# A residual accumulator loaded in four quarters, each at its own step, in the down projection of a transformer-like layer

## The chip, the cores and the metric

The kernel runs on one core of a Trainium2 chip. The core has a matrix engine (TensorE, PE in the profile), a vector engine (VectorE, DVE), a scalar engine (ScalarE, ACT), a general engine (GpSimd, POOL) and a queue engine (SyncE, SP) that issues transfers to sixteen DMA engines. Each engine runs its own list of instructions in order and waits on semaphores for the others. The metric is the device time of one execution in microseconds (us); lower is better.

## The reference, cut to what matters

One layer on 1024 tokens of 1024 channels. The mixing half (attention, a short convolution, a gated block) gives `h`; the change lies in the last lines, the second matrix product of the MLP and the final norm.

```python
x = x + jnp.einsum('bse,ed->bsd', mixed, w_out[l])          # h, 1024 x 1024
hdn = jnp.einsum('bsd,df->bsf', rms_norm(x, mlp_norm_g[l]), w_up[l])
hdn = jnp.square(jax.nn.relu(hdn))                           # 1024 x 4096
x = x + jnp.einsum('bsf,fd->bsd', hdn, w_down[l])            # the down stage
return rms_norm(x, final_norm_g)
```

## The kernel before

**Arithmetic.** Every fp32 product is made of three matmuls of split operands: each operand is written as a high and a low part (`split`, lines 51 to 53: ACT copies the high part, DVE subtracts to get the low part), and `mm3` (lines 63 to 66) adds high by high (L64), high by low of the moving operand (L65) and low of the stationary operand by high (L66).

**The down stage.** The up and down stages use a seven-product scheme (Winograd's form of Strassen) on two by two blocks. In the down stage the hidden layer's 4096 channels are cut into sixteen pairs of 128, and four blocks of four pairs; each block makes seven products in the order of `PLAN` (lines 1185 and 1186), so there are 28 steps. A step's product `m` takes 48 matmuls (4 groups of 128 tokens, 4 pairs, 3 matmuls each) in a PSUM bank of family A or B (`dA`, `dB` in the profile). After each group of tokens `u`, DVE adds the bank into a quarter of the accumulator (line 1220): `(i, k)` names the token half `i` (tiles 4i to 4i+3) and the column half `k` (512 columns). The first seven steps: steps 0 and 1 on quarter (0,0), step 2 (m=6) on (0,1), step 3 (m=5) on (1,1), step 4 (m=7) again on (1,1), step 5 (m=3) again on (0,1), step 6 (m=4) on (1,0).

**Accumulators.** `acc[t]`, eight tiles of 128 x 1024, start as `h`, which an earlier stage wrote to DRAM (`kept[t]`, named `hs` in the profile). `open_acc(t)` (lines 1125 to 1127) loads one tile whole, 512 KB.

**Operands of a step.** `down_ops(m, p)` (lines 1136 to 1154) loads one hidden operand `hr` (256 KB, from `hidden`, `hd..` in the profile), does the block's subtractions on the `w_down` rows `wd` where the product needs them (step 2, m=6: two per pair, `wd<-wd` and `t<-wd,wd`; m=7 and m=4: one), and splits both into `ho` and `wo`. Step 0's operands are made in the stage before. Step 1 needs only the odd rows of `w_down` (`load_down(BLOCKS[0], (1,))`, line 1196); step 2 is the first that needs the even ones. `hr` has 8 buffers, `wd` 10, `ho` and `wo` 10 each, so a new operand waits for the release of an older one.

**The order.** `prep(n + 1)`, the operands of the next step, stands ahead of step n's product in the program. A planner in the language then orders each engine's list ahead of the run by program order and by when it thinks an instruction could start; the SP queue gets its transfers in such an order too. In step 0's turn of the loop come, after `prep(1)`: four accumulator tiles, the even rows of `w_down` of block 0 (four transfers of 512 KB), the other four accumulator tiles, and the gain of the final norm, `gfin`, spread to all partitions (lines 1201 to 1207). `gfin` is first read in the last block (step 25, L1224). In step 4's turn `prep(5)` loads the rows of the second block.

Of the kernel before, what the change touches and what calls it, by code (L numbers as in the profile page):

```python
# [8 lines left out]
F32 = mybir.dt.float32  # L9
# [6 lines left out]
P = 128  # L16
T = 1024
D = 1024
# [12 lines left out]
def trunk(ctx, tc, x, mix_g, w_in, rb_rev, conv_w, sg_ln_g, sg_ln_b, sg_w, sg_b,  # L31
# [3 lines left out]
    load = nc.sync.dma_start  # L35
# [12 lines left out]
    def raw_tile(shape, name):  # L48
        return W.tile(shape, F32, tag="wr", bufs=3, name=name)
# [13 lines left out]
    def mm3(ps, sh, sl, mh, ml, start, stop, **kw):  # L63
        PE.matmul(ps, lhsT=sh, rhs=mh, start=start, stop=False, **kw)  # L64
        PE.matmul(ps, lhsT=sh, rhs=ml, start=False, stop=False, **kw)  # L65
        PE.matmul(ps, lhsT=sl, rhs=mh, start=False, stop=stop, **kw)  # L66
# [32 lines left out]
    def half(hf):  # L99
        return slice(hf * HALF, (hf + 1) * HALF)  # L100
# [49 lines left out]
    n = Rows("n", lambda hf, kp: "N")  # L150
# [3 lines left out]
    class Moving:  # L154
# [7 lines left out]
        def load(self, j):  # L162
            raw = self.raw[j] = raw_tile([P, self.kk, self.m], f"wr_{self.name}{j}")
            rows_ = slice(j * self.kk * P, (j + 1) * self.kk * P)
            load(raw, w_in[rows_, self.c0:self.c0 + self.m].rearrange("(k p) m -> p k m", p=P))
# [557 lines left out]
    for i in range(64):  # L723
        p, k = i // 16, i % 16
# [43 lines left out]
    def bank(name):  # L768
        return psB.tile([P, HALF], F32, tag="b", name=name)
# [49 lines left out]
    xn2, raws, spilled, kept = {}, {}, {}, {}  # L819
# [55 lines left out]
    def add(out, a, b):  # L875
        V.tensor_tensor(out, a, b, op=ALU.add)  # L876
# [127 lines left out]
    class Up:  # L1004
# [5 lines left out]
        def prep(self):  # L1010
            self.ops.raw()
            self.ops.sums()
            return self
# [105 lines left out]
    E_ = ctx.enter_context(tc.tile_pool(name="down", bufs=2, reuse_waits="tile"))  # L1119
    gfin = E_.tile([P, D], F32, tag="gfin", bufs=1, name="gfin")  # L1120
    BLOCKS = [tuple(range(i, i + 4)) for i in range(0, NP, 4)]
    acc = {}
    wd, t2 = {}, {}

    def open_acc(t):
        acc[t] = E_.tile([P, D], F32, tag="acc", bufs=8, name=f"acc{t}")
        load(acc[t], kept[t])

    def load_down(ps, rows=(0, 1)):
        for p in ps:  # L1130
            for i in rows:
                w = E_.tile([P, 2, HALF], F32, tag="wd", bufs=10, name=f"wd{p}{i}")
                load(w, w_down[(2 * p + i) * P:(2 * p + i + 1) * P, :].rearrange("p (k m) -> p k m", k=2))
                wd.setdefault(p, {})[i] = w
# [30 lines left out]
    def early_half(t, k):  # L1165
        square(t, k)
        V.tensor_scalar(sums[t][:, 2:3], sums[t][:, k:k + 1], 1.0 / D, EPS, op0=ALU.mult, op1=ALU.add)

    def finish(t, k):

        ss = sums.get(t)
        square(t, k)
        V.scalar_tensor_tensor(ss[:, 3:4], ss[:, k:k + 1], 1.0 / D, ss[:, 2:3], op0=ALU.mult, op1=ALU.add)  # L1173
        r = sm.tile([P, 1], F32, tag="rf", name="rf")
        G.tensor_tensor(r, ss[:, 3:4], mhalf[:, 0:1], op=ALU.pow)  # L1175
        o = E_.tile([P, D], F32, tag="o", bufs=2, name=f"o{t}")
        for i in (k, 1 - k):
            if t + 1 == NT and i != k:
                A.activation(o[:, half(i)], acc[t][:, half(i)], AF.Copy, scale=r)
            else:  # L1180
                V.scalar_tensor_tensor(o[:, half(i)], acc[t][:, half(i)], r, gfin[:, half(i)], op0=ALU.mult, op1=ALU.mult)
            load(out[t * P:(t + 1) * P, half(i)], o[:, half(i)])
# [15 lines left out]
    for n, (b, s) in enumerate(steps):  # L1198
        if n + 1 < len(steps):
            prep(n + 1)  # L1200
        if n == 0:
            for t in range(4):
                open_acc(t)
            load_down(BLOCKS[0], (0,))
            for t in range(4, 8):
                open_acc(t)
            load(gfin, fin_g.partition_broadcast(P))
        m, which, start, (i, k) = PLAN[s]
        ops = ready.pop(n)
        last = b == len(BLOCKS) - 1  # L1210
        for u in range(4):
            sl = slice(u * P, (u + 1) * P)
            if start:
                banks[which, u] = bank(f"d{which}{u}")
            ps = banks[which, u]
            for j, (ho, wo_) in enumerate(ops):
                mm3(ps, ho[:, 0, sl], ho[:, 1, sl], wo_[:, 0], wo_[:, 1], start and j == 0, j == len(ops) - 1,
                    skip_group_check=True)
            t = 4 * i + u
            add(acc[t][:, half(k)], ps, acc[t][:, half(k)])  # L1220
            if last and m in (2, 7):
                early_half(t, k)
            if last and m == 7 and t + 1 == NT:
                V.tensor_tensor(acc[t][:, half(k)], acc[t][:, half(k)], gfin[:, half(k)], op=ALU.mult)  # L1224
            if last and m in (3, 4):
                finish(t, k)
# [27 lines left out]
```

## Time and profile before

| what | value |
|---|---|
| median of 3 runs | 1130.63 us (1130.45 to 1135.13) |
| the profiled execution's own time | 1133.42 us |
| its span, first to last instruction | 1131.7 us |
| mean granted TensorE clock over the span | 0.989 of full |
| TensorE busy | 97% of the span |
| VectorE, ScalarE busy | 66%, 49% |

The profile is of one execution. Its own time is 2.79 us above the median of the three runs, and 1.72 us above its span. Clock is given as a share of 2.4 GHz: 1.00 is 2.4 GHz and 0.50 is 1.2 GHz. All times in the rows below are us from the start of the span.

### The profile page before, as it was taken

The numbers are of one execution on the slowest core, as the hardware profiler recorded it, in microseconds if no ns is written. First come the engines' busy times: TensorE is split into PE (matmuls) and PEld (weight loads), VectorE is DVE, ScalarE is ACT, GpSimd is POOL, SyncE is SP. The second block draws the span as 40 slices with busy tenths as digits, with TensorE's granted clock in tenths as the row PEclk, the third lists the DMA queues.
The fourth block names the chain that finished last, engine by engine and source line by source line (L and its number), as shares of the span: only waits on it lengthen the run. The fifth ranks groups of instructions, "written<-read, shape, count | busy, mean of one in ns | idle before, by whom it ended". The sixth has DMA issues, their size and how long they took to land.

```text
span 1131.7 us, 14984 instructions
## 1 busy us (share of the span) xinstructions
PE 1094.5 (97%) x5377; PEld 913.2 (81%) x5377; DVE 748.5 (66%) x1430; ACT 549.6 (49%) x1094; POOL 73.0 (6%) x131
## 2 busy tenths in 40 slices
PE   7999999999999999999999999999959999999996
PEld 6879987887888788887888888888748888888885
DVE  5526487667676752579756565655597968879775
ACT  5434375655664520566555555555343434334452
POOL 1101023111011200000000000000000000000001
PEclk9999999999999899999999999999989999999998
DMA  7523013021120143453535353535787255253303
GB/s 248 173 63 85 1 24 98 8 69 33 39 61 19 58 148 112 168 205 121 204 113 192 115 186 121 179 119 185 280 324 269 96 176 175 86 201 107 103 19 148
DMA packets 82045, 145.16 MB, mean 128 GB/s; under 512 B 5922, under 2 KB 41524, under 8 KB 81972
## 3 DMA queue, kind: packets, MB, share of 16 engines
q1 hardware_dynamic: 81396, 142.38, 37.5%
q10 hardware_dynamic: 576, 1.84, 0.4%
q8 instruction: 42, 0.69, 0.3%
q14 instruction: 31, 0.25, 0.1%
HBM read 98.58 MB, written 41.42 MB: 124 GB/s over the span
## 4 chain that ended last, share of the span: by engine, by line
PE 81%; DVE 8%; DMA 5%; ACT 2%; issue 2%; POOL 1%; SPq 0%; POOLq 0%; DVEq 0%; ACTq 0%
PE dA L64 5%; PE dA L66 5%; PE dA L65 4%; PE uA L66 4%; PE uA L65 4%; PE uA L64 4%; PE dB L64 3%; PE dB L66 3%; PE dB L65 3%; PE av L537 3%; PE uC L64 2%; PE uC L65 2%; PE o L64 2%; PE uC L66 2%; PE o L65 2%; PE o L66 2%
## 5 line engine op out<-in xcount | busy, mean ns | idle before, releaser
L52 ACT ACTIVATE ho<-hr 128x512 fp32r<-128x512 f32 x112 | 68.7, 621 | 156.7 <-PE dA L66 68.4
L64 PE MATMUL dA<-wo,ho 128*128 128x512 f32 x256 | 100.5, 392 | 11.4 <-ACT ho L52 11.4
L66 PE MATMUL dA<-wo,ho 128*128 128x512 f32 x256 | 100.3, 392 | 0.0
L65 PE MATMUL dA<-wo,ho 128*128 128x512 f32 x256 | 100.3, 392 | 0.0
L53 DVE TENSOR_TENSOR ho<-hr,ho 128x512 fp32r<-128x512 f32 x112 | 76.2, 685 | 20.3 <-ACT ho L52 20.3
L64 PE MATMUL dB<-wo,ho 128*128 128x512 f32 x192 | 74.9, 390 | 0.2 <-ACT ho L52 0.2
L66 PE MATMUL dB<-wo,ho 128*128 128x512 f32 x192 | 74.9, 390 | 0.0
L65 PE MATMUL dB<-wo,ho 128*128 128x512 f32 x192 | 74.7, 389 | 0.0
L53 DVE TENSOR_TENSOR wo<-wd,wo 128x512 fp32r<-128x512 f32 x96 | 65.0, 684 | 2.4 <-ACT wo L52 2.4
L64 PEld LDWEIGHTS dA<-wo,ho 128*128 128x128 f32 x256 | 48.6, 190 | 21.8 <-ACT ho L52 11.8
L52 ACT ACTIVATE wo<-wd 128x512 fp32r<-128x512 f32 x96 | 58.3, 616 | 5.8 <-DVE wd L879 2.3
L485 ACT ACTIVATE pr<-s,st 128x640 f32<-128x640 f32 (+2 forms) x64 | 42.2, 660 | 36.9 <-DVE st L480 26.6
L876 DVE TENSOR_TENSOR acc<-dA,acc 128x512 f32<-128x512 f32 x64 | 44.0, 688 | 20.2 <-PE dA L66 18.2
L66 PEld LDWEIGHTS dA<-wo,ho 128*128 128x128 f32 x256 | 48.4, 189 | 10.8 <-DVE ho L53 0.6
L65 PEld LDWEIGHTS dA<-wo,ho 128*128 128x128 f32 x256 | 48.5, 189 | 10.0
L510 ACT ACTIVATE pth<-pt 128x512 fp32r<-128x512 f32 (+2 forms) x96 | 39.9, 434 | 32.1 <-PE pt L506 31.4
L511 DVE TENSOR_TENSOR ptl<-pt,pth 128x512 fp32r<-128x512 f32 (+2 forms) x96 | 45.2, 486 | 12.8 <-ACT pth L510 11.9
L64 PE MATMUL o<-woh,mxh 128*128 128x512 f32 x128 | 50.7, 399 | 0.0
L66 PE MATMUL o<-woh,mxl 128*128 128x512 f32 x128 | 50.5, 394 | 0.0
L65 PE MATMUL o<-wol,mxh 128*128 128x512 f32 x128 | 50.4, 394 | 0.0
L1175 POOL TENSOR_TENSOR rf<-ssf,mhalf 128x1 f32<-128x1 f32 x8 | 4.4, 549 | 629.9 <-DVE ssf L1173 629.9
L876 DVE TENSOR_TENSOR hid<-uC,v 128x512 f32<-128x512 f32 x15 | 10.4, 692 | 51.6 <-PE uC L66 51.6
(344 smaller groups left out, 3082.2 us busy)
## 6 DMA issues: line engine op xcount, KB each, us to landing
wr_u<-in_w_up SPq DMA_DIRECT2D x32, 512.0 KB, 4.5
wd<-in_w_down SPq DMA_DIRECT2D x32, 512.0 KB, 5.1
wr_o<-in_w_out SPq DMA_DIRECT2D x8, 512.0 KB, 4.4
xr<-in_x SPq DMA_DIRECT2D x8, 512.0 KB, 4.9
hs<-h SPq DMA_DIRECT2D x8, 512.0 KB, 3.7
acc<-hs SPq DMA_DIRECT2D x8, 512.0 KB, 9.3
out_y<-o SPq DMA_DIRECT2D x16, 256.0 KB, 2.1
x<-in_x SPq DMA_DIRECT2D x7, 512.0 KB, 4.0
```

What stands on the lines that cost most here:

```text
L52: A.activation(hi, raw, AF.Copy)
L53: V.tensor_tensor(lo, raw, hi.bitcast(F32), op=ALU.subtract)
L64: PE.matmul(ps, lhsT=sh, rhs=mh, start=start, stop=False, **kw)
L65: PE.matmul(ps, lhsT=sh, rhs=ml, start=False, stop=False, **kw)
L66: PE.matmul(ps, lhsT=sl, rhs=mh, start=False, stop=stop, **kw)
L485: A.activation(pr[:, :b - a], s[:, a:b], AF.Exp, bias=st[:, 2:3], accum_out=lsum[p, t // 4][:, lc:lc + 1])
L510: A.activation(dh, src, AF.Copy)
L511: V.tensor_tensor(dl, src, dh.bitcast(F32), op=ALU.subtract)
L537: PE.matmul(dst, lhsT=lhs, rhs=rhs, start=first, stop=(i == len(kbs) - 1 and ph == 1))
L876: V.tensor_tensor(out, a, b, op=ALU.add)
L1175: G.tensor_tensor(r, ss[:, 3:4], mhalf[:, 0:1], op=ALU.pow)
```

## The change

Each accumulator tile is allocated as before but loaded by column halves of 256 KB. The four transfers of a quarter are issued in the turn of a step: quarter (0,0) in step 0's, (0,1) in step 2's, (1,1) in step 3's, (1,0) in step 5's (it is first added to in step 6). The load of `gfin` moves to step 14's turn. The even rows of `w_down` follow the first quarter directly.

```diff
-    def open_acc(t):
-        acc[t] = E_.tile([P, D], F32, tag="acc", bufs=8, name=f"acc{t}")
-        load(acc[t], kept[t])
+    def open_acc(i, k):
+
+        for t in range(4 * i, 4 * i + 4):
+            if t not in acc:
+                acc[t] = E_.tile([P, D], F32, tag="acc", bufs=8, name=f"acc{t}")
+            load(acc[t][:, half(k)], kept[t][:, half(k)])
@@
         if n == 0:
-            for t in range(4):
-                open_acc(t)
+            open_acc(0, 0)
             load_down(BLOCKS[0], (0,))
-            for t in range(4, 8):
-                open_acc(t)
+        elif n in (2, 3, 5):
+            open_acc(*{2: (0, 1), 3: (1, 1), 5: (1, 0)}[n])
+        elif n == 14:
             load(gfin, fin_g.partition_broadcast(P))
```

## Rows read from the trace of the kernel before

**Rows 1.** The page's busy table: engine, us, share, instructions.
```profile
PE 1094.5 (97%) x5377; PEld 913.2 (81%) x5377; DVE 748.5 (66%) x1430; ACT 549.6 (49%) x1094; POOL 73.0 (6%) x131
```
**Rows 2.** Windows of 20 us: length, busy us by engine, clock, DMA share, GB/s.
```profile
820.00:840.00 20.00, 8.60 (x29) 6.25 (x29) 19.40 (x33) 9.89 (x18) 0.00 (x0) 0.74 0.88 336
840.00:860.00 20.00, 20.00 (x90) 16.55 (x89) 15.54 (x26) 7.98 (x15) 0.00 (x0) 1.00 0.88 298
```
**Rows 3.** Waits of PE over the span: us in total, times, longest.
```profile
PE dA L64 <- ACT ho L52: 11.4, 1, 11.4
PE xT L218 <- DVE xn L231: 3.8, 1, 3.8
```
**Rows 4.** Timeline of PE: start, us, engine, line, operation, idle before.
```profile
823.66 0.39 PE L65 MATMUL dB<-wo,ho 128*128 128x512 f32 x1
823.89 0.39 PE L66 MATMUL dB<-wo,ho 128*128 128x512 f32 x1
...
835.68 0.80 PE L64 MATMUL dA<-wo,ho 128*128 128x512 f32 x1 [11.40 <-ACT ho L52]
...
840.34 0.40 PE L66 MATMUL dA<-wo,ho 128*128 128x512 f32 x1
```
**Rows 5.** Shorter windows around the gap, columns as in the 20 us windows.
```profile
829.00:829.50 0.50, 0.00 (x0) 0.00 (x0) 0.50 (x2) 0.50 (x2) 0.00 (x0) 1.00 1.01 401
829.50:830.00 0.50, 0.00 (x0) 0.00 (x0) 0.50 (x2) 0.50 (x2) 0.00 (x0) 0.51 0.99 385
...
840.00:842.00 2.00, 2.00 (x11) 1.63 (x10) 2.00 (x4) 1.17 (x2) 0.00 (x0) 1.00 0.82 227
```
**Rows 6.** Timeline of the SP queue: start of issue, us of issuing, transfer.
```profile
810.49 2.33 SPq L1127 DMA_DIRECT2D acc<-hs  x4
812.86 2.88 SPq L1133 DMA_DIRECT2D wd<-in_w_down  x4
816.52 4.15 SPq L1127 DMA_DIRECT2D acc<-hs  x4
821.63 0.33 SPq L1207 DMA_DIRECT2D gfin<-in_final_norm_g  x1
822.91 0.32 SPq L1139 DMA_DIRECT2D hr<-hd0c  x1
824.19 0.32 SPq L1139 DMA_DIRECT2D hr<-hd1c  x1
...
873.43 0.42 SPq L1133 DMA_DIRECT2D wd<-in_w_down  x1
```
**Rows 7.** DMA issues of single transfers: size, us from issue to landing.
```profile
hr<-hd3a SPq DMA_DIRECT2D x1, 256.0 KB, 4.0
...
wd<-in_w_down SPq DMA_DIRECT2D x1, 512.0 KB, 8.8
...
gfin<-in_final_norm_g SPq DMA_DIRECT2D x1, 512.0 KB, 10.2
...
hr<-hd0c SPq DMA_DIRECT2D x1, 256.0 KB, 9.6
...
hr<-hd1c SPq DMA_DIRECT2D x1, 256.0 KB, 9.0
```
**Rows 8.** Timeline of DVE from the first even row to the late operands.
```profile
821.64 0.69 DVE L879 TENSOR_TENSOR wd<-wd 128x512 f32<-128x512 f32 x1 [0.58 <-DMA wd<-in_w_down]
...
830.67 3.09 DVE L53 TENSOR_TENSOR wo<-wd,wo 128x512 fp32r<-128x512 f32 x5
833.68 1.88 DVE L879 TENSOR_TENSOR wd<-wd,wd 128x512 f32<-128x512 f32 x3
...
836.09 1.28 DVE L53 TENSOR_TENSOR ho<-hr,ho 128x512 fp32r<-128x512 f32 x2
```
**Rows 9.** Timeline of ACT, after the gap.
```profile
846.90 0.63 ACT L52 ACTIVATE ho<-hr 128x512 fp32r<-128x512 f32 x1 [4.81 <-PE dA L66]
...
857.78 0.63 ACT L52 ACTIVATE ho<-hr 128x512 fp32r<-128x512 f32 x1 [0.58 <-PE dB L66]
```

## The prediction

> **What bounds the kernel now.** I began with the busy table: TensorE is busy for 1094.5 of 1131.7 us [rows 1], so a change outside its path is worth at most what PE loses in the stage concerned. The windows of 20 us show one hole in the down stage: 820 to 840 has PE busy 8.60 us, at a mean clock of 0.74, followed by a full window, while DVE works 19.40 us and DMA runs at 0.88 of its time [rows 2]. The list of waits gives the hole one name: PE waited 11.4 us, once, at the first matmul of product 6 (step 2) for ACT's high part of the hidden operand; it is the longest wait of PE in the trace, the next is 3.8 us at the start [rows 3].
>
> The timeline of PE sizes the whole loss. Step 1's last matmul starts at 823.89, 0.23 us after the one before it, so the next would have started at 824.12. The next starts at 835.68. The clock was still full at 829.0 to 829.5, and half in the next half microsecond, after PE had stood idle for some 5.2 us since its end at 824.28; the window 840 to 842 is full again [rows 4, 5]. So the first matmuls of step 2 run slowly: its twelfth starts at 840.34. At 0.23 us each, eleven intervals are 2.53 us, and an undisturbed step would have had to start at 837.81 to be there. The hole costs 837.81 - 824.12 = 13.7 us: 11.6 from start to start and 2.1 of slow clock.
>
> Why is the operand late? The SP queue shows the order of the transfers: hidden operands of step 1, four accumulator tiles, the even `w_down` rows, four more tiles, `gfin`, and only then the hidden operands of step 2 (`hd0c`) [rows 6]. Issue plus time to landing: first even row 812.86 + 8.8 = 821.7, `gfin` 821.63 + 10.2 = 831.8, `hd0c` 822.91 + 9.6 = 832.5, `hd1c` 824.19 + 9.0 = 833.2 [rows 6, 7]. DVE agrees: it waited until 821.64 for the first even row [rows 8]. They land in issue order, so a transfer waits for the bytes ahead of it; with the queue full one of 512 KB takes (821.63 - 816.52) / 4 = 1.28 us, the spacing at which the second four tiles are issued as older ones land [rows 6].
>
> The second limiter is DVE's list. From 821.64 to its first low part of `ho` at 836.09 it is never idle; one instruction alone takes 0.69 us and five in a row 3.09, so one starts every 0.60 us, and the stretch holds 14.45 / 0.60 = 24 instructions [rows 8]. Only twelve are step 2's (for each of four pairs: two subtractions and one low part). The other twelve (two adds, four subtractions of step 4, six splits of later steps; the rows show three of these subtractions and five of these splits) stand ahead of the `ho` splits in an order that was planned with those transfers late.
>
> **The change part by part.** *Ahead of the even rows* stand four quarters of 256 KB in place of four tiles of 512 KB: 1 MB less. What does a half-size transfer cost? `hd0c` and `hd1c`, 256 KB each, land 833.2 - 832.5 = 0.7 us apart, against 1.28 for 512 KB [rows 6, 7]; I take 0.65, bounds 0.64 (half) and 0.75. So the first even row lands at 821.65 - 4 x (1.28 - 0.65) = 819.1, and the four at 819.1, 820.4, 821.7 and 823.0. Against this stands a rule of the Trainium skill, "DMA: Bandwidth & Descriptors", "Rules for kernel authors": for most bandwidth use 128 partitions and at least 1 MiB per transfer. The rows above show half size at half price with the queue full, so here it does not bite; where it would is a rival below.
>
> *Ahead of step 2's hidden operands* go the second four tiles (5.1 us) and `gfin` (1.3 us). After the last even row at 823.0 the four operands land at 0.65 us each: 823.7, 824.3, 825.0 and 825.6, some 9 us earlier than 832.5 and on. The issue wait on older transfers doesn't bind, since those are the small quarters, landed by 818.
>
> *DVE then is what PE waits for.* From 819.1 it must do step 2's sixteen instructions (two subtractions, two low parts, four pairs). Three adds of step 1 fall due meanwhile (PE ends it at 824.28), and I allow one instruction of fill, since the operands arrive right behind the rows: 20 x 0.60 = 12.0, so it ends at 831.1. Bounds: sixteen alone, 828.7; the same twelve fillers as before, 16 + 12 = 28 instructions, 835.9; and if DVE kept no queue, last landing 825.6, 0.63 on ACT [rows 9] and 0.68 on DVE, 826.9. The last low part of `ho` feeds the twelfth matmul, which starts when it is done; eleven intervals back, step 2 starts effectively at 831.1 - 2.53 = 828.6. PE's first matmul needs high parts alone and comes about 827 or before, so the idle time stays below the 5 us after which the clock fell [rows 5] and the slow 2.1 us goes too. Loss 828.6 - 824.12 = 4.5 us, gain 13.7 - 4.5 = 9.2 us.
>
> *The moved quarters.* They take the same bytes, 4 x 0.65 = 2.6 us of DMA each. Step 3's hidden operands land until 828.2, quarter (0,1) until 830.8; its first add is due when the first token group of step 2 ends, 828.6 + 12 x 0.23 = 831.4: free, by 0.6 us. Quarter (1,1) stands behind step 4's operands, which wait for buffers that DVE releases until 831.1; with eight transfers it lands by some 837, due at 842.2 (step 3's first group: 828.6 + 10.9 + 2.7). A step is 10.88 us, from the ACT releases 846.90 and 857.78 [rows 9]. Quarter (1,0) has two steps more. Cost nothing, covered by those margins; uncovered, a late quarter stops DVE with the splits behind it. `gfin` has eleven steps before its reader. The eight additional issues at 0.32 us are 2.6 us of SP, which here waits on landings anyway: nothing.
>
> *Does PE keep what it gains?* DVE loses the twelve instructions that it did during the stall. From 819.1 to step 4's twelfth matmul (828.6 + 21.8 + 2.5 = 852.9) it owes 16 + 8 + 12 operand instructions and 11 adds, 47 x 0.60 = 28.2 of 33.8 us. From step 4 on ACT's next operand waited for PE to end the step two before (846.90, 857.78, each released by PE's last matmul of a step [rows 9]), so this part follows PE, and PE fills the window behind the gap [rows 2]. The gain stays.
>
> **The rivals.** (a) *The gap closes fully.* DVE's fill moves behind the splits and 826.9 counts: start 824.4, gain 13.4, 1117.2 us. For: program order puts step 2's work first. Against: DVE's sum.
> (b) *DVE's list keeps its fill.* End 835.9, start 833.4, and PE idle for more than 5.2 us, so about 1.5 us of slow clock: gain 837.81 - 835.0 = 2.8, 1127.8. For: such an order was planned once. Against: that order fits late transfers.
> (c) *The smaller transfers carry a fixed price each.* If 256 KB cost 1.28 us as 512 KB do, the rows would stay at 821.65, DVE would end at 833.6 and step 2 start at 831.1: gain 837.81 - 831.1 - 1 of clock = 5.7, 1124.9 us. Nothing is left from some 2.5 us each: rows at 819.1 + 4 x 1.85 = 826.5, end 838.5, start 836.0, and the 2.1 of clock; 1130.9. Against: the 0.7 us between two landings [rows 6, 7]. By the Trainium skill, the same page, "Anatomy of one DMA — SWDGE (gpsimd) path", a fixed 2.0 us and the bytes at 436 GB/s make 2.6 us for 256 KB if nothing overlapped, an estimate that ends at no gain; it is fitted on another issue path, and no spacing here shows it.
> (d) *Slower: quarter (1,1) lands late.* It enters DVE's list at the adds of step 3, which with step 4's twelve operand instructions are sixteen, 9.6 us, due by 852.9: from a landing after 843.3 each us costs one, and at 852.5 the gain is gone. If the queue puts it behind the second block's eight row transfers, the last of them issued at 873.43 [rows 6], 9.2 earlier here, and it lands 4.0 us after its issue as `hd3a` did [rows 7], that is 868.2: 24.9 lost, 15.7 slower, 1146 us. Against: those loads stand one turn later in the program.
>
> **How the numbers follow.** The sum is of the profiled execution: 1133.42 - 9.2 = 1124.2; that execution lay 2.8 us over the median, and I take the gain off the median: 1130.63 - 9.2 = 1121.4 us. Chances: forecast 0.6 (range of its own 1118.5 to 1125); (a) 0.1; (b) 0.12; (c) 0.11, of which 0.03 with nothing left; (d) or another such wait 0.07. A measurement can tell about 0.5%, 5.65 us. Faster by more: 0.6 + 0.1 + 0.06 of (c) = 0.76; within: (b) and the rest of (c), 0.17; slower: 0.07. The range takes in (a), (b) and the first of (c), with about 1 us around them, and leaves out (d), (c) without gain and what I have not thought of: 1117 to 1129.
>
> **What would show it.** In the profile after: one PE wait at step 2 of about 3 us in place of 11.4; clock 1.00 throughout; the first even row landing near 819, the operands of step 2 near 824; DVE's first `ho` split for step 2 before 829; no DVE wait on an accumulator's transfer behind 820. The prediction is wrong if DVE still puts splits of later steps ahead of `ho`, if 256 KB transfers land over 0.8 us apart with the queue full, or if a wait of PE stands behind step 2.

## The result, and the profile after

The changed kernel takes 1118.44 us (median of 4 runs, 1116.98 to 1118.95); the kernel before, run beside it, 1130.99 us (4 runs, 1130.45 to 1135.13). The ratio is 0.9873, with a 95% interval of 0.9857 to 0.9889: 12.6 us faster where 9.2 were forecast. The profiled execution took 1118.65 us, with a span of 1116.9 us.

The windows of 20 us of the changed kernel, columns as in [rows 2]:

```profile
820.00:840.00 20.00, 18.75 (x81) 14.54 (x80) 20.00 (x34) 12.02 (x22) 0.00 (x0) 1.00 0.84 311
840.00:860.00 20.00, 20.00 (x90) 16.55 (x89) 18.08 (x31) 10.07 (x17) 0.00 (x0) 1.00 0.86 299
```

TensorE (PE) is busy for 18.75 us where it was for 8.60, at full clock, and the window behind is as full as it was. VectorE (DVE) is busy throughout. In PE's list of waits the 11.4 us at step 2 have become two small ones; the first row is now PE's longest wait in the whole trace, where it was the second before [rows 3]:

```profile
PE xT L218 <- DVE xn L231: 4.2, 1, 4.2
...
PE dA L64 <- ACT ho L52: 0.8, 1, 0.8
...
PE dA L66 <- DVE ho L53: 0.5, 1, 0.5
```

PE's timeline, from step 1's last matmul over the start of step 2 (bank family `dA`) to step 3's first (`dB`), answers to [rows 4]:

```profile
820.76 0.39 PE L66 MATMUL dB<-wo,ho 128*128 128x512 f32 x1
821.93 0.50 PE L64 MATMUL dA<-wo,ho 128*128 128x512 f32 x1 [0.78 <-ACT ho L52]
822.27 0.40 PE L65 MATMUL dA<-wo,ho 128*128 128x512 f32 x1
822.51 0.40 PE L64 MATMUL dA<-wo,ho 128*128 128x512 f32 x1
822.75 0.40 PE L65 MATMUL dA<-wo,ho 128*128 128x512 f32 x1
823.62 0.73 PE L66 MATMUL dA<-wo,ho 128*128 128x512 f32 x2 [0.47 <-DVE ho L53]
...
828.50 0.62 PE L65 MATMUL dA<-wo,ho 128*128 128x512 f32 x2
...
833.95 0.39 PE L64 MATMUL dB<-wo,ho 128*128 128x512 f32 x1
```

**One measure for the hole.** In what follows the loss of step 2 is the start of step 3's first matmul, less the moment at which step 2 could have begun (the start of step 1's last matmul plus 0.23), less the 10.88 us of a step. Here that is 833.95 - 820.99 - 10.88 = 2.1 us. Before, step 3 began at 848.75, and the loss was 848.75 - 824.12 - 10.88 = 13.75 us. So the hole gave 11.7 us. The row is from PE's timeline of the kernel before:

```profile
848.75 0.39 PE L64 MATMUL dB<-wo,ho 128*128 128x512 f32 x1
```

The two spans differ by 14.8 us; of that 2.3 us were there before the down stage (the first odd `w_down` rows are issued at 787.89, against 790.23 before), where both kernels have the same code, and 0.8 us arose from there to step 1's last matmul (33.66 us before, 32.87 after), a stretch that took from 32.87 to 34.04 us in e1 to e4 below, with the same code in its path. From step 3's first matmul to the end both take the same 282.95 us: 1131.7 - 848.75 and 1116.9 - 833.95. Nothing is lost later. A time of this trace plus 824.12 - 820.99 = 3.1 us is the like time of the trace before.

The SP queue, columns as in [rows 6]:

```profile
807.57 0.32 SPq L1142 DMA_DIRECT2D hr<-hd3a  x1
807.94 1.85 SPq L1130 DMA_DIRECT2D acc<-hs  x4
809.84 2.71 SPq L1136 DMA_DIRECT2D wd<-in_w_down  x4
812.59 0.64 SPq L1142 DMA_DIRECT2D hr<-hd0c  x1
814.11 0.33 SPq L1142 DMA_DIRECT2D hr<-hd1c  x1
814.78 0.32 SPq L1142 DMA_DIRECT2D hr<-hd2c  x1
815.45 0.32 SPq L1142 DMA_DIRECT2D hr<-hd3c  x1
816.77 0.32 SPq L1142 DMA_DIRECT2D hr<-hd0c  x1
818.04 0.32 SPq L1142 DMA_DIRECT2D hr<-hd1c  x1
...
821.24 2.36 SPq L1130 DMA_DIRECT2D acc<-hs  x4
...
827.58 2.10 SPq L1130 DMA_DIRECT2D acc<-hs  x4
829.72 13.45 SPq L1136 DMA_DIRECT2D wd<-in_w_down  x6
```

Step 2's hidden operands (the first `hd0c` to `hd3c`) are issued directly behind the even rows. With the queue full each issue waits for an older landing, so the spacing shows the price of what lands: 0.67 us (814.11, 814.78, 815.45) while the 256 KB quarters do, 1.27 us (816.77, 818.04) while the 512 KB rows do. The first even row lands 6.9 us after its issue, at 816.74. DVE from there to step 2's last operand:

```profile
816.73 0.69 DVE L879 TENSOR_TENSOR wd<-wd 128x512 f32<-128x512 f32 x1
...
822.87 0.69 DVE L53 TENSOR_TENSOR ho<-hr,ho 128x512 fp32r<-128x512 f32 x1
...
827.09 0.69 DVE L876 TENSOR_TENSOR acc<-dB,acc 128x512 f32<-128x512 f32 x1
827.69 0.69 DVE L53 TENSOR_TENSOR wo<-t,wo 128x512 fp32r<-128x512 f32 x1
```

Nineteen instructions start from 816.73 to 827.69: step 2's sixteen and three adds of step 1, no split of a later step. The last ends at 828.38, which is 831.5 in the time of the trace before; 831.1 was forecast. So the last operand came when it was forecast to come, and PE still lost 2.1 us and not 4.5. The order in which PE takes its matmuls explains it. From each kernel's list of PE, the first matmuls of step 2 (pairs p0 to p3; each token group adds into a bank of its own, dA0 to dA3):

```
before   dA0: pair 0 L64 L65 L66, pair 1 L64 L65 L66, pair 2 ..., pair 3 (10th to 12th); then dA1 ...
after    dA0 p0 L64 L65 | dA1 p0 L64 L65 | dA0 p0 L66 | dA1 p0 L66 | dA0 p1 L64 L65 | dA1 p1 L64 L65 | dA2 p0 L64 ...
         first matmul of pair 3: the 21st; first that reads its last low part (L65): the 26th
```

The planner ordered PE's list anew: it works on three token groups with the pairs that are there. It is the second of the two L65 at 828.50, at 828.73, that reads the part ready at 828.38, so PE no longer waits for it. What PE does wait for are pair 0's parts: 0.78 us for ACT's high part at the first matmul, and 0.47 us at the fifth for the low part that DVE finishes at 822.87 + 0.69 = 823.56.

### The profile page after: what moved, and what is told of

It reads as the page before. It is cut to its first block, busy times and chain, and to the rows that moved or that the text cites. A ratio compares the mean times of both kernels' runs of the same rounds, so it can differ in the third digit from the quotient of the medians.

```text
span 1116.9 us, 14983 instructions
## 1 busy us (share of the span) xinstructions
PE 1090.4 (98%) x5377; PEld 911.8 (82%) x5377; DVE 746.9 (67%) x1430; ACT 551.5 (49%) x1094; POOL 73.2 (7%) x131
## 4 chain that ended last, share of the span: by engine, by line
PE 85%; DVE 7%; DMA 4%; ACT 2%; issue 1%; POOL 0%; SPq 0%; POOLq 0%; DVEq 0%; ACTq 0%
PE uA L66 5%; PE uA L65 5%; PE uA L64 5%; PE dA L66 5%; PE dA L64 5%; PE dA L65 4%; PE dB L64 3%; PE dB L66 3%; PE dB L65 3%; PE av L537 3%; PE uC L64 2%; PE uC L66 2%; PE uC L65 2%; PE o L64 2%; PE o L65 2%; PE o L66 2%
## 5 line engine op out<-in xcount | busy, mean ns | idle before, releaser
L65 PE MATMUL dA<-wo,ho 128*128 128x512 f32 x256 | 99.5, 389 | 0.0
L65 PE MATMUL dB<-wo,ho 128*128 128x512 f32 x192 | 74.7, 389 | 0.0
L65 PEld LDWEIGHTS dA<-wo,ho 128*128 128x128 f32 x256 | 48.1, 188 | 9.9
L511 DVE TENSOR_TENSOR ptl<-pt,pth 128x512 fp32r<-128x512 f32 (+2 forms) x96 | 45.2, 487 | 12.9 <-ACT pth L510 11.9
L65 PE MATMUL o<-wol,mxh 128*128 128x512 f32 x128 | 50.0, 390 | 0.0
```

The costliest lines, as they stand in the source:

```text
L511: V.tensor_tensor(dl, src, dh.bitcast(F32), op=ALU.subtract)
```

## The experiments

Three theories. **Bytes:** the hole was the 3.5 MB in the queue ahead of step 2's operands, and each part of it counts by its transfers. **Order:** the planner's new order of PE makes the difference between 4.5 and 2.1 us of loss. **Order alone:** PE's order would have helped the kernel before too. e1 to e4 ran on one chip, c_after and e5 to e7 on a second, those with f_ on a third, each group beside the kernel before (1133.38, 1133.23 and 1133.18 us). Losses are from one profiled execution each.

| kernel | us | ratio to before, 95% | loss of step 2, us |
|---|---|---|---|
| before | 1130.99 | 1 | 13.75 |
| after (first comparison) | 1118.44 | 0.9873 (0.9857 to 0.9889) | 2.1 |
| e2_gfin | 1131.62 | 0.9985 (0.9970 to 1.0000) | 12.4 |
| e1_whole | 1124.37 | 0.9932 (0.9911 to 0.9952) | 4.2 |
| e3_strict, f_strict | 1123.72, 1123.66 | 0.9923 (0.9905 to 0.9940), 0.9914 (0.9895 to 0.9932) | 5.1, 4.2 |
| c_after, f_after (the change again) | 1121.34, 1121.22 | 0.9889 (0.9869 to 0.9908), 0.9888 (0.9870 to 0.9907) | 1.8, 1.3 |
| e4_rows | 1120.53 | 0.9897 (0.9879 to 0.9914) | 1.6 |
| e5_pairs, f_pairs | 1120.54, 1120.48 | 0.9894 (0.9876 to 0.9913), 0.9883 (0.9862 to 0.9903) | 0.5, 0.4 |
| e7_128k | 1121.94 | 0.9903 (0.9887 to 0.9919) | 4.1 |
| e6_first | 1128.54 | 0.9962 (0.9947 to 0.9978) | 0, but 8 ahead of step 1 |
| f_before_pairs | 1134.21 | 1.0002 (0.9988 to 1.0015) | 13.6 |

**Only `gfin` moved (e2_gfin).** The kernel before, with one line more:

```diff
             for t in range(4, 8):
                 open_acc(t)
+        elif n == 14:
             load(gfin, fin_g.partition_broadcast(P))
```

> The kernel before with only gfin moved to step 14's turn. Theory: 1.3 us less ahead of the hidden operands of step 2, the same order on DVE and PE otherwise: a gain of 0 to 1.3 us, ratio 0.999 to 1.000. Rival (the planner's order flips with any shift of the transfers): several us faster.

The loss fell from 13.75 to 848.48 - 825.23 - 10.88 = 12.4 us: 1.4 us, near the 1.28 of one 512 KB transfer. By time, no gain is clear of the noise. PE's wait in the timeline of e2_gfin:

```profile
833.68 0.79 PE L64 MATMUL dA<-wo,ho 128*128 128x512 f32 x1 [8.29 <-ACT ho L52]
```
The stretch of DVE's timeline that ends it:

```profile
831.56 3.09 DVE L53 TENSOR_TENSOR wo<-wd,wo 128x512 fp32r<-128x512 f32 x5
834.57 0.68 DVE L879 TENSOR_TENSOR wd<-wd,wd 128x512 f32<-128x512 f32 x1
835.18 0.68 DVE L53 TENSOR_TENSOR ho<-hr,ho 128x512 fp32r<-128x512 f32 x1
```

Five splits and two subtractions of later steps still stand ahead of the first `ho` split, where the kernel before had six and four. So most of the fill stayed, but not all, and PE now waits a second time, 1.0 us at its third matmul; that the 1.4 us are the transfer's price alone is not shown.

**`gfin` and the second four tiles moved, tiles whole (e1_whole).** As e2_gfin, and also:

```diff
             load_down(BLOCKS[0], (0,))
+        elif n == 3:
             for t in range(4, 8):
                 open_acc(t)
```

> Whole tiles as before the change, but tiles 4 to 7 load in step 3's turn and gfin in step 14's; the halves are left out. Theory (what counts is the bytes ahead of step 2's operands, 1 MB more here than in the changed kernel): the first even row lands 2.5 us later than in the changed kernel, DVE and step 2 follow by 2.5, so about 1121 us, a ratio to the kernel before of 0.991; matmuls of step 2 still interleaved by the planner. Rival (the halves and the per-product placing are the point): most of the gain is lost, 1127 or more. Second rival (only what leaves the queue between the rows and the hidden operands counts): 1118.5.

The loss fell to 839.55 - 824.50 - 10.88 = 4.2 us, 8.2 less than with `gfin` alone and 2.1 above the whole change, where 2.5 were expected. DVE's first `ho` split for step 2 starts at 828.26, ahead of the splits of later steps, so four tiles less turned DVE's order too; PE's list takes the token groups together, as after the change. What is left, in PE's timeline of e1_whole:

```profile
824.27 0.39 PE L66 MATMUL dB<-wo,ho 128*128 128x512 f32 x1
827.18 0.79 PE L64 MATMUL dA<-wo,ho 128*128 128x512 f32 x1 [2.52 <-ACT ho L52]
...
829.90 0.47 PE L66 MATMUL dA<-wo,ho 128*128 128x512 f32 x1
```
The clock (third figure from the right) in windows of half a microsecond:

```profile
826.00:826.50 0.50, 0.00 (x0) 0.00 (x0) 0.50 (x2) 0.50 (x1) 0.00 (x0) 1.00 1.04 385
826.50:827.00 0.50, 0.00 (x0) 0.00 (x0) 0.50 (x2) 0.50 (x2) 0.00 (x0) 0.64 1.05 385
...
829.50:830.00 0.50, 0.50 (x3) 0.40 (x2) 0.50 (x2) 0.50 (x3) 0.00 (x0) 0.50 0.50 111
830.00:830.50 0.50, 0.50 (x4) 0.41 (x3) 0.50 (x2) 0.50 (x3) 0.00 (x0) 0.94 0.82 209
```

From 827.18 to 829.90 six matmuls take 2.72 us in place of 1.36: the clock is at half until 830. Of the 2.1 us that the halves ahead of the even rows bring over this kernel, 1.4 are this slow clock, which does not occur after the whole change.

**PE in program order (e3_strict, f_strict).** The changed kernel, with PE's list held to the program's order in step 2:

```diff
+        one = ExitStack()
+        if n == 2:
+            one.enter_context(tc.manual_schedule(engines={mybir.EngineType.PE}))
         for u in range(4):
...
+        one.close()
```

> The changed kernel with step 2's matmuls held in program order on PE (one token group after the other, four pairs each). Theory (the forecast missed because PE's list interleaves token groups while later pairs are made): the loss at step 2 rises from 2.1 us to the forecast 4.5, time about 1120.9, 2.4 above the changed kernel. Rival (the operands themselves came earlier than forecast, the order on PE does not matter): 1118.5, loss 2.1.

> Step 2's matmuls in program order again, now beside the changed kernel on one chip. Theory (the planner's interleaving of token groups on PE is the term that the forecast left out): loss 4.8 to 5.3 us, time 3 us above the changed kernel. Rival (the order is worth less than 1 us, the first run's difference came from the chip): within 1 us of it.

The loss is 5.1 and 4.2 us (in both, three of step 3's matmuls slipped in among step 2's, and 51 intervals are taken off in place of 48), against 2.1, 1.8 and 1.3 with the planner's order. On one chip f_strict takes 2.4 us more than f_after by the medians (1123.66 and 1121.22), but the intervals of the ratios overlap; by the profiles its loss is 2.9 us greater. The operands did not move: in e3_strict DVE's timeline has the same instructions at the same times as after the change, from the first even row to the last operand:

```profile
816.73 0.69 DVE L879 TENSOR_TENSOR wd<-wd 128x512 f32<-128x512 f32 x1
...
827.69 0.68 DVE L53 TENSOR_TENSOR wo<-t,wo 128x512 fp32r<-128x512 f32 x1
```
PE's timeline of f_strict:

```profile
825.06 0.39 PE L66 MATMUL dB<-wo,ho 128*128 128x512 f32 x1
825.74 0.50 PE L64 MATMUL dA<-wo,ho 128*128 128x512 f32 x1 [0.29 <-ACT ho L52]
826.07 0.40 PE L65 MATMUL dA<-wo,ho 128*128 128x512 f32 x1
827.42 0.50 PE L66 MATMUL dA<-wo,ho 128*128 128x512 f32 x1 [0.95 <-DVE ho L53]
...
841.06 0.39 PE L65 MATMUL dB<-wo,ho 128*128 128x512 f32 x1
```

PE stands at the third matmul for a low part that the planner's order asks for two matmuls later. The forecast's 4.5 us lies between the two losses. Most of what e3_strict loses beyond f_strict is clock, as its windows of half a microsecond show:

```profile
826.00:826.50 0.50, 0.50 (x3) 0.24 (x1) 0.50 (x2) 0.23 (x1) 0.00 (x0) 0.60 1.06 389
...
829.00:829.50 0.50, 0.50 (x3) 0.40 (x2) 0.50 (x2) 0.50 (x2) 0.00 (x0) 0.50 1.03 385
829.50:830.00 0.50, 0.50 (x3) 0.42 (x3) 0.50 (x2) 0.50 (x2) 0.00 (x0) 0.98 0.90 320
```
The five intervals from the first matmul of pair 3 on take 2.32 us there (827.29 to 829.61) and 1.56 in f_strict (831.09 to 832.65), whose clock stayed at 1.00.

**Pairs outermost (e5_pairs, f_pairs).** The changed kernel; in step 2 PE takes all four token groups with pair 0, then pair 1, and so on:

```diff
+        if n == 2:
+            with tc.manual_schedule(engines={mybir.EngineType.PE}):
+                for j, (ho, wo_) in enumerate(ops):
+                    for a, b in ((0, 0), (0, 1), (1, 0)):
+                        for u in range(4):
+                            PE.matmul(banks[which, u], lhsT=ho[:, a, u * P:(u + 1) * P], rhs=wo_[:, b], start=False, ...)
...
-            for j, (ho, wo_) in enumerate(ops):
+            for j, (ho, wo_) in enumerate(() if n == 2 else ops):
```

> The changed kernel with step 2's matmuls held in another order on PE: pair after pair, and for each pair the four token groups' high by high, then high by low, then low by high. Theory (what is left of the loss is PE's list waiting for a pair that DVE has not finished): a pair feeds twelve matmuls, 2.7 us, and DVE makes one in 2.4 and the adds between, so only the start of the first pair remains; loss 0.9 to 1.2 us in place of 2.1, time 1 us below the changed kernel. Rival (DVE's rate sets it in any order): loss 2 us, same time.

> Pair after pair, operation after operation in step 2 again, beside the changed kernel. Theory: loss 0.4 to 0.7 us, time 1.3 us below the changed kernel. Rival (what PE gains there is lost in a later step): same time, with a wait of PE behind step 2.

The 48 matmuls of f_pairs run without a gap, in PE's timeline:

```profile
824.82 11.17 PE L1219 MATMUL dA<-wo,ho 128*128 128x512 f32 x48
835.83 0.39 PE L64 MATMUL dB<-wo,ho 128*128 128x512 f32 x1
```

Losses of 0.5 and 0.4 us, below the 0.9 to 1.2 first expected. The times, 0.8 and 0.7 us below the changed kernel on the same chip, lie inside the intervals: this is the version with the least loss, but its times do not part from the changed kernel's.

The traces part the orders more sharply. Call lead the time from DVE's first subtraction for step 2 to the moment at which step 2 could have begun; it differs between executions. Lead and loss together are 6.3, 6.4 and 6.3 us in the three profiles of the changed kernel (leads 4.26, 4.61 and 5.07), 8.9 us in f_strict (4.75; 9.7 in e3_strict, with its slow clock) and 5.35 us in both with pairs outermost (4.86 and 4.99). So the program's order costs 2.6 us against the planner's, pairs outermost save 1.0, and the spread of 1.3 to 2.1 follows the lead.

**The same order in the kernel before (f_before_pairs).**

> The kernel before with its transfers as they are, and only step 2's matmuls pair after pair. Theory (the transfers and DVE's list bound to them are the cause; the order on PE only matters once they come early): PE still waits 10 us or more for ACT's first high part, the clock still falls; gain 0 to 1.5 us, ratio 0.9985 to 1.000. Rival (the order on PE is the larger part): 5 us or more faster.

PE's timeline, with all of step 2 in one row:

```profile
835.94 13.62 PE L1216 MATMUL dA<-wo,ho 128*128 128x512 f32 x48 [10.89 <-ACT ho L52]
```

PE waits nearly as long (10.89 us for 11.40), and the time is the same (1.0002). Order alone gives nothing while the first operand is late.

**The change again (c_after, f_after).** Nothing is edited.

> The changed kernel itself, once more, as the mark for the kernels beside it. Both theories: a ratio to the kernel before of 0.987 to 0.990; loss at step 2 in the profile 2.1 us as in its first profile.

> The changed kernel beside the two with another order on PE, on one chip. Both theories: loss at step 2 of 1.7 to 2.1 us in the profile, as in its two profiles so far.

Ratios of 0.9889 and 0.9888 agree with the first 0.9873 within the intervals; the losses are 1.8 and 1.3 us where 2.1 and 1.7 to 2.1 were expected.

**Even rows ahead of the quarter (e4_rows).** The changed kernel with two lines exchanged:

```diff
         if n == 0:
-            open_acc(0, 0)
             load_down(BLOCKS[0], (0,))
+            open_acc(0, 0)
```

> The changed kernel with the even rows issued ahead of the first quarter. Theory (DVE's work on step 2 starts when the first even row lands and PE follows it): rows land 2.6 us earlier, the adds of steps 0 and 1 wait for their quarter until after the rows; PE's loss at step 2 falls from 2.1 to between 0.5 and 1.2 us, time 1117 us. Rival (the adds of step 0, now late, stand in DVE's list ahead of the subtractions): no gain or 1 us slower than the changed kernel, 1118.5 to 1119.5.

DVE's first subtraction for step 2 starts at 814.16 in place of 816.73, but the quarter's own adds of step 0 now come later, four in a row at 821.45, among step 2's work, and the hidden operands are issued from 816.06 on, behind the quarter. Loss 835.49 - 823.04 - 10.88 = 1.6 us, within the 1.3 to 2.1 of the changed kernel and above the 0.5 to 1.2 expected: with the quarter's adds and the hidden operands now later, taking 1 MB from ahead of the rows gained nothing.

**Even rows ahead of step 1's operands (e6_first).** The changed kernel; they follow the odd rows, ahead of the loop:

```diff
     load_down(BLOCKS[0], (1,))
+    load_down(BLOCKS[0], (0,))
...
             open_acc(0, 0)
-            load_down(BLOCKS[0], (0,))
```

> The changed kernel with the even rows issued right behind the odd ones, ahead of step 1's hidden operands. Theory (transfers ahead of step 2 are the cause, and DMA has idle time before 805): the rows land by 808, DVE's subtractions run during steps 0 and 1, the hidden operands of step 2 land 5 us earlier; loss at step 2 below 0.5 us, time 1.5 to 2 us below the changed kernel. Rival (the rows hold up step 1's hidden operands or wait for buffers of the stage before): PE waits before step 1 instead, 0 to 5 us slower than the changed kernel.

Step 2 then starts without loss, but the SP queue shows the price:

```profile
788.07 23.09 SPq L1136 DMA_DIRECT2D wd<-in_w_down  x8
811.21 0.43 SPq L1142 DMA_DIRECT2D hr<-hd0a  x1
```
PE's timeline, at the start of step 1:

```profile
817.87 0.80 PE L64 MATMUL dB<-wo,ho 128*128 128x512 f32 x1 [8.02 <-ACT ho L52]
```

The eight row loads hold SP for 23.09 us, where four took 6.40, and step 1's operands stand behind them: `hd0a` is issued at 811.21, after the change at 800.67. PE waits 8.0 us one step earlier, and its clock is at 0.50 from 816 to 820. The kernel takes 7.2 us more than c_after, beyond the 5 us of the rival. In this queue a load whose buffer is not free blocks every transfer behind it.

**Quarters in pieces of 128 KB (e7_128k).** The changed kernel, each half row in two transfers of 256 columns:

```diff
-            load(acc[t][:, half(k)], kept[t][:, half(k)])
+            for c in range(k * HALF, (k + 1) * HALF, 256):
+                load(acc[t][:, c:c + 256], kept[t][:, c:c + 256])
```

> The changed kernel with each quarter's rows in two transfers of 128 KB in place of one of 256 KB (32 accumulator loads in place of 16). Theory (a transfer costs its bytes when the queue is full): the first even row lands within 0.3 us of where it does in the changed kernel, time within 0.5 us of it. Rival (each transfer carries a fixed price): four more ahead of the rows at 0.6 to 2 us each, rows and step 2 later by 2.5 to 8 us, 1121 to 1126 us.

The SP queue of e7_128k:

```profile
809.88 3.92 SPq L1131 DMA_DIRECT2D acc<-hs  x8
813.85 2.02 SPq L1137 DMA_DIRECT2D wd<-in_w_down  x4
```
DVE's timeline, at the first even row:

```profile
820.55 0.69 DVE L879 TENSOR_TENSOR wd<-wd 128x512 f32<-128x512 f32 x1 [2.45 <-DMA wd<-in_w_down]
```

Eight issues take 0.49 us each, and the rows are issued 4.3 us after `hd3a` (809.51) in place of 2.3. DVE waits 2.45 us for them, PE 2.2 us at step 2, and the clock falls: loss 838.69 - 823.74 - 10.88 = 4.1 us. The DMA engines show 0.90 of their time in 816 to 820, against 1.02 after the change. The first even row lands 6.7 us after its issue (820.55 - 813.85), after the change 6.9, so it is late because it is issued late: here SP's issuing sets the pace, not the bytes. The profiled execution, the slowest of the four, shows 2.3 us more loss than c_after; the times of the two, 1121.94 and 1121.34, do not part.

## Why the prediction came out as it did

**Right: what the hole was, and that it would go.** With the 3.5 MB out of the way PE's long wait is gone, the clock is full throughout the stage, and the 282.95 us behind are unchanged, so the gain is kept. The parts, by loss of step 2 and in the order in which they were added: `gfin` 1.4 us, the second four tiles 8.2 (with them DVE's and PE's order turned), the halves 2.1.

**Right: half size at half price.** Issues 0.67 us apart as the quarters land; 0.65 was taken. Rival (c) is out for 256 KB. The rule of at least 1 MiB per transfer (the Trainium skill, "DMA: Bandwidth & Descriptors", "Rules for kernel authors") does not show at this size. The 128 KB pieces show a price of each transfer: SP's 0.49 us of issue, which is more than the 0.34 that half of 0.67 would be.

**Right, in part by luck: DVE's sum.** Twenty instructions from 819.1 to 831.1 were forecast; it was nineteen, from 819.9 to 831.5 in that time. The first even row came 0.8 us later than forecast and DVE did one instruction less, and the two nearly cancel. Rival (b) is out after the change. Its order is real: most of it stands in e2_gfin, where the transfers are late still.

**Wrong in size: "The last low part of `ho` feeds the twelfth matmul, which starts when it is done; eleven intervals back, step 2 starts effectively at 831.1 - 2.53 = 828.6."** The step read PE's order off the program and off the list of the kernel before. I had allowed the planner a new order of DVE, and not of PE. In its new order the last low part is a `wo` one, first read by the 26th matmul, 25 intervals of 0.23 us behind the start, so it would have allowed a start at 828.38 - 25 x 0.227 = 822.7. Pair 0's low part, read by the fifth matmul at 823.62, gives the same: 823.62 - 4 x 0.227 = 822.7, and this is a part that PE waited for. So 822.7 - 820.99 = 1.7 us of the 2.1 are lost to it; the rest is in slower intervals behind the waits (0.34 us, as from 821.93 to 822.27). The term, loss 4.5 us, measured 2.1, 1.8 and 1.3 in three profiles. Held to the order that I had assumed, with DVE's list unchanged, the kernel loses 4.2 us, and 5.1 with the clock at half for a while. That settles this step: the gain at the hole is 11.7 to 12.5 us in place of 9.2, and the medians (12.6 in the first comparison, 11.9 and 12.0 in the others) agree.

**Rival (a)** forecast nearly the time, by another mechanism: it wanted all of step 2's operands by 826.9. They came at 831.5, and the gap closed because PE asked for them later.

**Right, and not tried: the moved quarters cost nothing.** (0,1) is issued from 821.24 and lands 5.3 us after issue; with the groups interleaved its adds start only at 833.10. (1,1) is issued at 827.58, ahead of the second block's rows at 829.72, and lands 4.9 us after issue. No DVE wait behind 820 is put down to an accumulator's transfer. Rival (d) needed that order turned round; no run did that, so its price stays an estimate.

**Half right: "the idle time stays below the 5 us after which the clock fell".** The slow clock did go, with waits of 0.8 and 0.5 us. But 5 us was no bound: in e1_whole and e7_128k the clock fell with waits of 2.5 and 2.2 us, and in e3_strict, which has the order that I had assumed, with none above 0.94 us; in f_strict, with the same order, it did not fall. Had PE waited the 3 us that I expected, slow clock would probably have come on top, 1.4 us by e1_whole.

## What to carry to other kernels

Count the bytes that stand in the queue ahead of a late operand, and move those that are read steps later: whole transfers that need not be there gave most of this gain, their size little. Where a planner orders the engines' lists, a transfer that comes earlier changes the order in which every engine takes its work, the consumer's too, so ask of each late operand how far down the consumer's list its first reader can stand. With several accumulating groups open, taking the operand that is there through all groups leaves the next one the time to arrive.

## What the runs showed of the hardware that was not expected

- TensorE's clock fell to 0.50 some 2.0 us after PE's end in e1_whole (end 824.66, mean 0.64 in 826.5 to 827.0), where 5.2 us had passed in the kernel before [rows 5]. In e7_128k, idle from 823.90 to 826.09, PE was at work again when it fell, at about 826.6. In e3_strict it fell at about 826.1 after waits of 0.45, 0.94 and 0.49 us with matmuls between them; in f_strict waits of 0.29, 0.95, 0.49 and 0.66 us brought no fall, nor did 0.78 and 0.47 us after the change. So PE's longest wait alone does not tell whether the clock falls. In e1_whole full clock was back by 830.5, 3.3 us after PE's first matmul.
- One transfer's issue on SP took 0.32 us alone, and 0.46 (the four quarters, 1.85 us) to 0.49 us (eight pieces) in a row. For 256 KB that is less than the 0.67 us in which one lands behind another; for 128 KB it is more than half of that (an estimate, as no 128 KB spacing was measured with the queue full).
